# Differential attention on one core: two maps on the two halves of the array, one pass over the probabilities, the 16 prefix keys as a full chunk

## The chip, the cores and the metric

The kernel runs on one core of a Trainium2 chip. The metric is the device time of one execution in microseconds (us). TensorE (PE in the rows) does the matrix products, and its weight loads are listed apart as PEld; VectorE is DVE, ScalarE is ACT, GpSimd is POOL, SyncE is SP. The time before is 3174.17 us, the median of three runs.

## The reference, cut to what matters

The program is a hybrid block of three kinds of attention with a convolutional feed-forward layer, followed by two layers of a second kind. Each of the two layers has a SwiGLU, a mixing sublayer and another SwiGLU. The change touches the mixing sublayer's differential attention, on 16 prefix ("meta") tokens and 512 tokens, four heads, two maps of 64 features per head and values of 128 features:

```
s = einsum('bhmid,bhmjd->bhmij', q, k) * scale      # m = 0, 1: the two maps
p = softmax(where(allowed, s, -1e30))               # causal
a = p[:, :, 0] - lam * p[:, :, 1]
o = einsum('bhij,bhje->bhie', a, v)
o = o * rsqrt(mean(o * o) + EPS) * subln_w * (1 - lambda_init)
```

## The kernel before

The program is written against a layer that places buffers, adds the semaphores and puts the instructions of each engine in an order of its own: an instruction goes into its engine's order when, by that planner's own clock, its operands and its buffer are there, and among those that are ready the one written earlier in the program goes first. So matrix products written later (the projections of the next heads) are placed between the attention's own steps wherever those wait. Once the order is fixed, each engine takes its instructions in it.

PSUM has eight banks, in four rings: four banks "g" (projections), two "s" (scores), one "t" (transposes) and one "o" (outputs of the values' product).

`mix` handles a layer's mixing sublayer. It computes the four heads' values (`v_heads`, `v_major`), and then for b = 0 and 1 the queries and keys of two heads each: `gemm` (L172) makes a projection from exact high and low parts of both operands, with three products for each row block of 128 and the tokens in two segments of 264 (of one segment of 512 for the last layer's queries); `rotate` applies the rotary table; `stack` cuts the result into parts. Each b ends with `diff_heads` over its two heads, so that there are four such stages in the program, two for each layer. After them come the retention heads' projections, which are also L172.

`stack` makes tiles for products that are 128 deep. For map m (64 rows) the queries' high part and low part lie one above the other; for the keys the high part lies there twice, and one more tile holds the low parts of both maps. So a map's scores are one product 128 deep (L1466) and one 64 deep (L1467).

`diff_block` treats 128 queries (block b = 1 to 4, with 16 + 128 b keys; b = 0 is the 16 prefix tokens, which the last layer leaves out). For each map: the two products, the causal mask added by an identity product in bf16 (L1469), the row maximum (L1471), its scaling (L1476), the exponential with row sums (L1478). Block 4 has 528 keys, over the 512 of a bank, so its keys are taken in two spans of 264, each with a bank and the two products. Then two reciprocals (L1484, L1485), a pass that scales map 1 (L1486) and one that combines the maps (L1489). `yield`s part the steps: the generator of `diff_heads` writes scores(i + 1), transposes(i), values(i - 1). The transposes of the chunks of 128 keys go to bank "t" (L1496) and are copied in one piece (L1497); the 16 prefix keys are transposed into bank "o" (L1500) and copied apart (L1501). The values' product takes the chunks 128 deep (L1503), the prefix keys 16 deep (L1504); in f32 each of these is two matmul instructions. L1505 copies the result out and L1507 sums its squares.

Over the program there are 8 heads of a layer: 24 blocks b = 1 to 3, 8 blocks b = 4, and 4 blocks b = 0.

Of the kernel before, what the change touches and what calls it, by code (L numbers as in the profile page):

```python
# [10 lines left out]
F32 = mybir.dt.float32  # L11
# [54 lines left out]
class Weights:  # L66
    """[128, 512] tiles (high, low) of a [K, c] block, 512 / c rows of 128 in each"""
# [17 lines left out]
class QWeights:  # L85
    """tiles of the quarters (column tile n, rows k < 4 or k >= 4)"""
# [8 lines left out]
class Builder:  # L95
# [80 lines left out]
    def strassen_y(self, ys, R, keep=False):  # L176
        """the sums of the quarters of y (rows k < 4 and k >= 4, first and second half of the tokens)"""
# [17 lines left out]
    def gemm_pairs(self, W, ys, R, use, between=()):  # L195
        """all column tiles; the first two advance together, as the last of ys may come late"""
# [24 lines left out]
    def y_sums(self, T, k, a, c, w, q4, pool=None):  # L221
        """a and c: the rows k < 4 and k >= 4 of the first half of the tokens; w: both of the second half"""
# [25 lines left out]
    def strassen(self, src, Y, R, out, last, off=0, mid=None):  # L248
        """[2 * 128 features, tokens] of a block of weights with seven products of quarters (Winograd's form);
        the last product lies among the next block's, and last takes what it gives"""  # L250
# [15 lines left out]
        def product(i, ps=None, tag="g"):  # L266
            """with ps, added to what is there"""
# [59 lines left out]
    def sumsq(self, acc, src, R, k):  # L327
        """acc += src^2"""
# [27 lines left out]
    def bcast(self, rc, R):  # L356
        """rc, a column for each chunk of tokens, as rows in all partitions"""
# [34 lines left out]
    def prenorm_r(self, R):  # L392
        """the reciprocal of the norm, in all partitions"""
# [24 lines left out]
    def halves(self, parts, products, post, nextw, nparts=None):  # L418
        """the last products before a norm, half of the tokens by half; the second half is normalised in the next phase"""
# [53 lines left out]
    def bias_table(self, kind):  # L473
        """each row 128 times, to be read along its diagonals"""
# [22 lines left out]
    def band_head(self, qT, kT, base, kbase, V, bias, ops, obase, negm, l, sink=None):  # L497
        """q^T, k^T [64 rows, 512] in natural order; V(kb) the [128, 64] block; previous and own block."""
# [36 lines left out]
    def block_head(self, qT, kT, base, V, bias, ops, negm, l):  # L535
        """four independent 128-blocks"""
# [28 lines left out]
    def v_direct(self, W, ys, rcol, d):  # L565
        """values token-major: block b holds tokens b*128.. (d=1) or b::4 (d=4)"""
# [15 lines left out]
    def v_transposed(self, vTs, bufs=3):  # L582
        """[128 features, 512] tiles -> token-major blocks"""
# [82 lines left out]
    def gates(self, Y, gates):  # L666
        """the gates' products, kept in DRAM until the branches are merged"""
# [11 lines left out]
    def post_tile(self, ps, acc, t, R, add):  # L679
        """collects a tile of the sublayer's output, in the place of x, and its squares"""  # L680
# [8 lines left out]
    def postnorm(self, acc, gpost, R, Rn, xold, xnew):  # L689
        """x = xold + norm(x); the next pre-norm of the tokens Rn"""  # L690
# [186 lines left out]
    def stick_pair(self, q, k, V, t, ops, tri, cm):  # L877
        """two heads; the blocks j of 128 keys against the queries from j*128 on lie one after the other"""
# [71 lines left out]
    def conv_ffn(self):  # L950
# [5 lines left out]
        def conv(u, j):  # L956
            """u holds two zeros before the first token"""
# [84 lines left out]
    def last_w(self, src, nk=4, spare=("t3",)):  # L1042
        """nk rows of 128 for all columns, in two blocks; what the ring doesn't hold lies where the sums of y were"""
# [19 lines left out]
    def ffn_order(self, chunks, up, down, last):  # L1063
        """the down products of a chunk lie between the up products of the next one"""
# [15 lines left out]
    def flush(self):  # L1080
        """the elementwise rest of a block follows the products of the next one"""
# [4 lines left out]
    def hidden(self, src, dst):  # L1086
        """the parts of two hidden tiles"""
# [7 lines left out]
    # ---------------------------------------------------------------- block 2  # L1095
# [91 lines left out]
    def first_blocks(self, name, ys, R, gs):  # L1187
        """the first blocks in halves of the tokens, so that the second half has time to be normalised"""
# [27 lines left out]
    def mix(self, l, R):  # L1216
# [3 lines left out]
        with self.phase(f"mx{l}") as qp:  # L1220
# [22 lines left out]
            for b in range(2):  # L1243
                wq = wi(2 + 2 * b)
                q = [self.stack(self.rotate(self.gemm(wq, n, ys, R), rot, True), R, False) for n in range(2)]
# [3 lines left out]
                k = [self.stack(self.rotate(self.gemm(wk, n, ys, R2), rot, True), R2, True) for n in range(2)]  # L1249
# [74 lines left out]
    def feature_major(self, o, base, R):  # L1324
        """transposes [tokens, 128] blocks; yields (psum, first token, tokens) within the range R"""
# [27 lines left out]
    def lam(self, l):  # L1353
        nc = self.nc
# [9 lines left out]
        nc.vector.scalar_tensor_tensor(out=e[:, 2:3], in0=e[:, 0:1], scalar=li, in1=e[:, 1:2], op0=ALU.add, op1=ALU.subtract)  # L1364
# [32 lines left out]
    def stack(self, t, R, key):  # L1397
        """the two maps' exact parts for products of K = 128: the queries' high and low parts against the keys' high
        part twice, and the high part against the keys' low part"""
        nc = self.nc  # L1400
        s = slice(R.off, R.off + R.n)
        r = [slice(0, 64), slice(64, P)]
        out = [self.tmp("qk2", 10, dt=F32R) for _ in range(2)]
# [299 lines left out]
```

## Time and profile before

| | us |
|---|---|
| median of the three runs (lowest, highest) | 3174.17 (3173.94, 3175.4) |
| the profiled execution's span, first to last instruction | 3173.5 |
| PE busy in it | 3105.4 |
| DVE busy | 2250.6 |
| ACT busy | 1533.8 |

The profiled execution shows its span; the time of a run is what lies between its first and last instruction and a little around them, and the median of the runs is 0.7 us over this span. Busy time of PE counts an instruction from its start to its modelled end, and a matmul's end lies after the next one's start, so that a lost tenth of a microsecond between two matmuls does not show as idle time. It shows in the distance from one start to the next, which the timeline gives.

### The profile page before, as it was taken

To read this page: it belongs to the slowest core of one execution; us is meant where nothing else is said; L and a number is where in the kernel's file an instruction comes from. 1 tells how busy PE (TensorE), PEld (TensorE's weight loads), DVE (VectorE), ACT (ScalarE), POOL (GpSimd) and SP (SyncE) were. 2 spreads that over 40 slices of the span, in tenths; PEclk is the share of its full clock that TensorE was granted. 3 is DMA by queue.
4 is the path that set the end of the run, shared out by engine and by line. 5 is a ranking of instruction groups with operands and counts; after the bars stand their busy time and mean duration, and the time that the engine had idled before them with its cause. 6 is when DMAs were issued, how large, how long until landed. Compare 5 with 4: busy or idle time off the path is not lost.

```text
span 3173.5 us, 54811 instructions
## 1 busy us (share of the span) xinstructions
PE 3105.4 (98%) x22264; PEld 2872.8 (91%) x22264; DVE 2250.6 (71%) x4225; ACT 1533.8 (48%) x2968; POOL 0.7 (0%) x6
## 2 busy tenths in 40 slices
PE   5899999999999999999999999999999999999998
PEld 4676798988899999999889999999999988899998
DVE  4235777887888797775766777768777576677775
ACT  3345555665455554444553444445444455344443
POOL 0000000000000000000000000000000000000000
PEclk8899999999999999999999999999999999999999
DMA  4421236423233332333212223333233321223332
GB/s 120 95 78 62 81 123 204 145 87 111 89 102 110 102 107 94 107 98 104 66 52 64 87 88 106 94 100 94 94 107 95 107 67 59 67 84 106 96 108 77
DMA packets 102148, 304.36 MB, mean 96 GB/s; under 512 B 12387, under 2 KB 27367, under 8 KB 101896
## 3 DMA queue, kind: packets, MB, share of 16 engines
q1 hardware_dynamic: 98296, 294.38, 30.0%
q10 hardware_dynamic: 3600, 6.49, 0.7%
q8 instruction: 174, 2.85, 0.4%
q14 instruction: 78, 0.64, 0.1%
HBM read 286.41 MB, written 14.42 MB: 95 GB/s over the span
## 4 chain that ended last, share of the span: by engine, by line
PE 93%; DMA 4%; DVE 2%; ACT 1%; issue 0%; SPq 0%; DVEq 0%; ACTq 0%
PE ps_g L172 35%; PE ps_g L278 18%; PE ps_g L276 9%; PE ps_s L172 8%; PE ps_g L206 7%; PE ps_o L276 4%; PE ps_o L206 1%; DMA fd<-row 1%; PE ps_g L576 1%; DMA wraw<-in_w_in 1%; PE ps_s L1467 1%; DMA tmp_bias<-fd 1%; PE ps_s L510 1%; PE ps_s L1524 1%; PE ps_o L1503 1%; PE ps_o L532 1%
## 5 line engine op out<-in xcount | busy, mean ns | idle before, releaser
L140 DVE TENSOR_TENSOR wqL<-wraw,wqH 128x512 fp32r<-128x512 f32 (+1 forms) x676 | 604.8, 910 | 275.3 <-ACT wqH L139 267.4
L139 ACT CAST wqH<-wraw 128x512 fp32r<-128x512 f32 (+1 forms) x676 | 526.7, 796 | 495.6 <-PE ps_g L172 258.6
L172 PE MATMUL ps_g<-yH,wqH 128*128 128x264 f32 (+2 forms) x1520 | 430.4, 322 | 2.3 <-ACT wqH L139 2.2
L172 PE MATMUL ps_g<-yL,wqH 128*128 128x264 f32 (+2 forms) x1520 | 430.8, 321 | 0.4 <-DVE yL L414 0.4
L172 PE MATMUL ps_g<-yH,wqL 128*128 128x264 f32 (+2 forms) x1520 | 430.3, 322 | 0.8 <-DVE wqL L140 0.7
L278 PE MATMUL ps_g<-t,wqH 128*128 128x256 f32 (+1 forms) x1760 | 326.5, 283 | 0.0
L172 PEld LDWEIGHTS ps_g<-yL,wqH 128*128 128x128 f32 x1520 | 264.7, 189 | 24.9 <-issue 5.2
L172 PEld LDWEIGHTS ps_g<-yH,wqL 128*128 128x128 f32 x1520 | 263.1, 189 | 23.4 <-issue 4.1
L172 PEld LDWEIGHTS ps_g<-yH,wqH 128*128 128x128 f32 x1520 | 263.4, 189 | 22.6 <-ACT wqH L139 3.1
L278 PEld LDWEIGHTS ps_g<-t,wqH 128*128 128x128 f32 x1760 | 272.4, 188 | 1.8
L278 PE MATMUL ps_g<-t,wqL 128*128 128x256 f32 (+1 forms) x880 | 248.7, 283 | 0.0
L139 ACT CAST wqH<-ws 128x1024 fp32r<-128x1024 f32 x100 | 105.2, 1052 | 126.8 <-PE ps_o L276 34.3
L278 PEld LDWEIGHTS ps_g<-t,wqL 128*128 128x128 f32 x880 | 166.1, 189 | 0.0
L276 PE MATMUL ps_g<-t,wqH 128*128 128x264 f32 (+1 forms) x800 | 148.5, 283 | 0.0
L172 PE MATMUL ps_s<-hL,wqH 128*128 128x264 f32 (+1 forms) x544 | 141.4, 317 | 0.0
L172 PE MATMUL ps_g<-hL,wqH 128*128 128x264 f32 (+1 forms) x544 | 141.3, 317 | 0.0
L172 PE MATMUL ps_g<-hH,wqL 128*128 128x264 f32 (+1 forms) x544 | 141.2, 317 | 0.0
L172 PE MATMUL ps_s<-hH,wqL 128*128 128x264 f32 (+1 forms) x544 | 141.2, 317 | 0.0
L172 PE MATMUL ps_g<-hH,wqH 128*128 128x264 f32 (+1 forms) x544 | 141.1, 317 | 0.0
L172 PE MATMUL ps_s<-hH,wqH 128*128 128x264 f32 (+1 forms) x544 | 141.0, 317 | 0.0
L258 DVE TENSOR_TENSOR ws<-wraw 128x512 f32<-128x512 f32 x100 | 69.3, 693 | 86.9 <-DMA wraw<-in_ffn_w_gate 34.7
L140 DVE TENSOR_TENSOR wqL<-ws,wqH 128x1024 fp32r<-128x1024 f32 x100 | 122.4, 1224 | 6.6 <-ACT wqH L139 3.1
(434 smaller groups left out, 8207.9 us busy)
## 6 DMA issues: line engine op xcount, KB each, us to landing
wraw<-in_ffn_w_gate SPq DMA_DIRECT2D x88, 512.0 KB, 3.7
wraw<-in_ffn_w_up SPq DMA_DIRECT2D x88, 512.0 KB, 3.7
wraw<-in_ffn_w_down SPq DMA_DIRECT2D x88, 512.0 KB, 3.5
wraw<-in_w_in SPq DMA_DIRECT2D x86, 512.0 KB, 3.8
wraw<-in_w_up SPq DMA_DIRECT2D x64, 512.0 KB, 3.7
wraw<-in_w_down SPq DMA_DIRECT2D x32, 512.0 KB, 3.5
wraw<-in_w_gate SPq DMA_DIRECT2D x24, 512.0 KB, 4.1
tmp_p<-gates ACTq DMA_DIRECT2D x24, 256.0 KB, 3.6
```

The lines of the kernel that those rows point to most:

```text
L139: self.nc.scalar.copy(out=H, in_=raw)
L140: self.nc.vector.tensor_sub(out=L, in0=raw, in1=H.bitcast(F32))
L172: self.nc.tensor.matmul(t[:, :m], lhsT=a, rhs=b[:, o:o + m], start=(k == 0 and i == 0), stop=(k == nk - 1 and i == 2))
L206: self.nc.tensor.matmul(q[:, :m], lhsT=a, rhs=b[:, o:o + m], start=(k == 0 and i == 0), stop=(k == nk - 1 and i == 2))
L258: nc.vector.tensor_add(out=S[:, :512], in0=A21, in1=A22)
L276: nc.tensor.matmul(ps, lhsT=a, rhs=b, start=first, stop=last)
L278: nc.tensor.matmul(ps, lhsT=a, rhs=b, start=False, stop=last, skip_group_check=True)
L510: nc.tensor.matmul(ps[:, c], lhsT=q[:, i * P:(i + 1) * P], rhs=k[:, lo * P:(i + 1) * P], start=True, stop=True)
L532: nc.tensor.matmul(ops[obase:obase + 64, i * P:(i + 1) * P], lhsT=V(kb), rhs=pT[:, s0:s0 + P], start=(kb == lo), stop=(kb == i))
L576: nc.tensor.matmul(ps[:, :256], lhsT=a[:, ts], rhs=w, start=(k == 0 and i == 0), stop=(k == KD - 1 and i == 2))
L1467: nc.tensor.matmul(ps[:nq, :e - a], lhsT=qm[r], rhs=k[2][r, a:e], start=False, stop=not dg)
L1503: nc.tensor.matmul(ops[:nq, :P], lhsT=aT[:, j * P:j * P + nq], rhs=V[:, j], start=(j == 0), stop=False)
```

## The change

- `parts` takes the place of `stack`: a tile of high parts and one of low parts for queries and for keys, map 0 in rows 0 to 63 and map 1 in rows 64 to 127, each made by one instruction of ACT and one of DVE over all 128 rows. The queries are multiplied by the scale there.
- The scores of a map are three products 64 deep. The program writes them by turns for the two maps: high by high for map 0, then for map 1, low by high for both, high by low for both; the masks of both come after them.
- Block 4's spans are 512 keys and the 16 prefix keys. The first takes the two banks "s", the second two banks of the ring "g".
- Both row maxima are taken with a negated output, so that the scaling instruction goes; the combination of the spans' maxima and sums and the reciprocals treat both maps in one instruction.
- The maps are combined in one pass, a = p0 - (lam * l0 / l1) * p1, with l the row sums, and the result is divided by l0 when it leaves PSUM.
- The prefix keys become a chunk of 128 whose values are zero beyond row 15 (`memset` on POOL in `v_major`); it is the first 128 columns of the probabilities, transposed with the others into bank "t" and copied in the same piece (for block 4 into bank "o", copied apart).

```diff
-                q = [self.stack(self.rotate(self.gemm(wq, n, ys, R), rot, True), R, False) for n in range(2)]
+                q = [self.parts(self.rotate(self.gemm(wq, n, ys, R), rot, True), R, SCALE) for n in range(2)]
...
-                k = [self.stack(self.rotate(self.gemm(wk, n, ys, R2), rot, True), R2, True) for n in range(2)]
+                k = [self.parts(self.rotate(self.gemm(wk, n, ys, R2), rot, True), R2) for n in range(2)]
...
+    def parts(self, t, R, scale=None):
+
+        H, L = [self.tmp("qk2", 10, dt=F32R) for _ in range(2)]
+        self.split(t, H, L, R.off, R.n, scale)
+        return H, L
...
         out = self.qp.tile([P, 5, P], F32, name="vh", tag="vh", bufs=6)
+        nc.gpsimd.memset(out[:, 4], 0.0)
...
-        spans = [(0, nk)] if nk <= 512 else [(0, nk // 2), (nk // 2, nk)]
+        spans = [(0, nk)] if nk <= 512 else [(NMETA, nk), (0, NMETA)]
...
+        for i, (a, e) in enumerate(spans):
+            ps = [self.psum("sg"[i])[:nq, :e - a] for _ in range(2)]
+            for j, (x, y) in enumerate(((0, 0), (1, 0), (0, 1))):
+                for m in range(2):
+                    nc.tensor.matmul(ps[m], lhsT=q[x][r[m], qs], rhs=k[y][r[m], a:e], start=(j == 0),
+                                     stop=(j == 2 and i == 1))
+            if i == 0:
+                for m in range(2):
+                    nc.tensor.matmul(ps[m][:, e - a - nq:], lhsT=self.identb[:nq, :nq], rhs=self.dm[:nq, :nq],
+                                     start=False, stop=True)
+            pst.append(ps)
+        for i, ps in enumerate(pst):
+            for m in range(2):
+                c = 2 * i + m
+                nc.vector.tensor_reduce(out=sm[:nq, c:c + 1], in_=ps[m], axis=AX.X, op=ALU.max, negate=True)
...
+        nc.vector.reciprocal(out=sm[:nq, 8:10], in_=sm[:nq, 4:6])
+        nc.vector.scalar_tensor_tensor(out=sm[:nq, 10:11], in0=sm[:nq, 4:5], scalar=sm[:nq, 9:10], in1=lam[:nq],
+                                       op0=ALU.mult, op1=ALU.mult)
         a = Pm[0]
-        nc.vector.scalar_tensor_tensor(out=a[:nq, :nk], in0=a[:nq, :nk], scalar=sm[:nq, 8:9], in1=Pm[1][:nq, :nk],
-                                       op0=ALU.mult, op1=ALU.subtract)
+        nc.vector.scalar_tensor_tensor(out=a[:nq, :nk], in0=Pm[1][:nq, :nk], scalar=sm[:nq, 10:11], in1=a[:nq, :nk],
+                                       op0=ALU.mult, op1=ALU.add)
...
-                nc.tensor.transpose(pt[:, j * P:j * P + nq], a[:nq, NMETA + j * P:NMETA + (j + 1) * P], self.ident[:nq, :nq])
-            nc.scalar.copy(out=aT[:, :b * P], in_=pt[:, :b * P])
+                nc.tensor.transpose(pt[:, j * P:(j + 1) * P], a[:, NMETA + j * P:NMETA + (j + 1) * P], self.ident)
+            if b < 4:
+                nc.tensor.transpose(pt[:, b * P:(b + 1) * P], a[:, :P], self.ident)
+            n = min(b + 1, 4) * P
+            nc.scalar.copy(out=aT[:, :n], in_=pt[:, :n])
...
-        nc.tensor.matmul(ops[:nq, :P], lhsT=aT[:16, 4 * P:4 * P + nq], rhs=V[:16, 4], start=(b == 0), stop=True)
-        nc.vector.tensor_copy(out=o_sb[:nq, b], in_=ops[:nq, :P])
+        kk = 16 if b == 0 else P
+        nc.tensor.matmul(ops[:nq, :P], lhsT=aT[:kk, m], rhs=V[:kk, 4], start=(b == 0), stop=True)
+        nc.vector.tensor_scalar(out=o_sb[:nq, b], in0=ops[:nq, :P], scalar1=sm[:nq, 8:9], scalar2=None, op0=ALU.mult)
```

## Rows read from the trace of the kernel before

**Rows 1.** The page: busy time by engine, granted clock, chain that ended last.
```profile
PE 3105.4 (98%) x22264; PEld 2872.8 (91%) x22264; DVE 2250.6 (71%) x4225; ACT 1533.8 (48%) x2968; POOL 0.7 (0%) x6
...
PEclk8899999999999999999999999999999999999999
...
PE 93%; DMA 4%; DVE 2%; ACT 1%; issue 0%; SPq 0%; DVEq 0%; ACTq 0%
```

**Rows 2.** Windows: stretch, length, busy and (instructions) of PE, PEld, DVE, ACT, POOL; clock, DMA.
```profile
1495.00:1532.50 37.50, 37.50 (x316) 37.42 (x314) 21.86 (x37) 14.88 (x27) 0.00 (x0) 1.00 0.25 85
1532.50:1587.00 54.50, 54.17 (x366) 44.69 (x365) 44.39 (x138) 35.34 (x108) 0.00 (x0) 1.00 0.18 58
1587.00:1640.00 53.00, 53.00 (x358) 43.35 (x358) 36.70 (x127) 28.87 (x104) 0.00 (x0) 1.00 0.14 43
...
2564.40:2615.00 50.60, 50.49 (x299) 39.95 (x297) 41.26 (x118) 32.93 (x95) 0.00 (x0) 1.00 0.19 63
2615.00:2665.00 50.00, 50.00 (x332) 40.96 (x331) 32.84 (x106) 26.19 (x89) 0.00 (x0) 1.00 0.12 38
```

**Rows 3.** Timeline of PE around block 4's scores of map 1: start, length, instruction.
```profile
1608.35 0.40 PE L172 MATMUL ps_g<-yH,wqL 128*128 128x264 f32 x2
1608.59 0.28 PE L172 MATMUL ps_g<-yH,wqH 128*128 128x264 f32 x1
1608.71 0.28 PE L1466 MATMUL ps_s<-tmp_qk,tmp_qk 128*128 128x264 f32 x1
1608.92 0.39 PE L1467 MATMUL ps_s<-tmp_qk,tmp_qk 64*128 64x264 f32 x1
1609.24 0.39 PE L172 MATMUL ps_g<-yH,wqH 128*128 128x264 f32 x1
1609.46 0.28 PE L172 MATMUL ps_g<-yL,wqH 128*128 128x264 f32 x1
1609.58 0.28 PE L1466 MATMUL ps_s<-tmp_qk,tmp_qk 128*128 128x264 f32 x1
```

**Rows 4.** Timeline of PE: transposes, and a block's values with the 16-deep product.
```profile
1552.62 0.66 PE L1503 MATMUL ps_o<-vh,tmp_aT 128*128 128x128 f32 x4
1553.21 0.48 PE L1504 MATMUL ps_o<-vh,tmp_aT 16*128 16x128 f32 x2
1553.62 0.51 PE L172 MATMUL ps_g<-yH,wqL 128*128 128x264 f32 x2
1553.97 0.41 PE L172 MATMUL ps_g<-yH,wqH 128*128 128x264 f32 x2
...
1555.07 0.49 PE L1496 MATMUL ps_t<-ident,tmp_P 128*128 128x128 f32 x3
1555.40 0.27 PE L1500 MATMUL ps_o<-ident,tmp_P 128*16 128x128 f32 x1
```

**Rows 5.** Timeline of PE in the first block: 64-deep products of heads on alternate halves.
```profile
164.57 1.71 PE L543 MATMUL ps_s<-qk 64*128 64x128 f32 x16
166.50 1.16 PE L543 MATMUL ps_s<-qk 64*128 64x128 f32 x8 [0.23 <-DVE tmp_p L545]
```

**Rows 6.** Timeline of ACT: the exponentials that free the banks of rows 3.
```profile
1607.52 0.46 ACT L1478 ACTIVATE tmp_P<-ps_s,sm 128x264 f32<-128x264 f32 x1
...
1607.97 0.47 ACT L1478 ACTIVATE tmp_P<-ps_s,sm 128x264 f32<-128x264 f32 x1
```

**Rows 7.** One line's instructions: the projection's evacuation by ACT and DVE, the 64-deep weight loads.
```profile
L1385 ACT COPY tmp_t<-ps_g x28: 351/378/587, 1514.8 to 2615.2; 128x264 f32<-128x264 f32 x24, 128x512 f32<-128x512 f32 x4
...
L1392 DVE TENSOR_TENSOR tmp_sg<-ps_g,rot x28: 411/424/674, 1515.2 to 2618.0; 128x264 f32<-128x264 f32 x24, 128x512 f32<-128x512 f32 x4
...
L1467 PEld LDWEIGHTS ps_s<-tmp_qk,tmp_qk x88: 88/183/184, 1532.7 to 2655.5; 64*128 64x128 f32 x80, 64*16 64x16 f32 x8
```

**Rows 8.** Groups by line, 1532 to 1640 us, and POOL's memset in the whole program.
```profile
L1471 DVE TENSOR_REDUCE sm<-ps_s 128x1 f32<-128x264 f32 (+4 forms) x48 | 18.6, 388 | 13.6 <-PE ps_s L1469 10.0 <-PE ps_s L1467 3.4
...
L1486 DVE TENSOR_SCALAR tmp_P<-tmp_P,sm,lame 16x16 f32<-16x16 f32 (+4 forms) x20 | 8.2, 412 | 0.2
...
L1407 ACT CAST tmp_qk<-tmp_sg 64x528 fp32r<-64x528 f32 x11 | 6.9, 631 | 3.2 <-DVE tmp_sg L1394 3.0
...
masks.py:197 POOL MEMSET ident<- 128x128 f32 x1 | 0.2, 204 | 0.3 <-POOLq L1692 0.3
```

More of the change, by code (lines that the diff above doesn't have):

```diff
@@ L1363, in lam @@
         nc.scalar.activation(out=e[:, :2], in_=ps[:, :2], func=AF.Exp)
[L1364 removed]
+        nc.vector.scalar_tensor_tensor(out=e[:, 2:3], in0=e[:, 1:2], scalar=-li, in1=e[:, 0:1], op0=ALU.add, op1=ALU.subtract)
         return e[:, 2:3]
@@ L1395, in rotate @@
         return out
[L1397 to L1403, printed above, removed]
-        low = self.tmp("qk2", 10, dt=F32R) if key else None
-        for m in range(2):
-            a, b = r[m], r[1 - m]
-            nc.scalar.copy(out=out[m][a, s], in_=t[a, s])
-            if key:
-                nc.scalar.copy(out=out[m][b, s], in_=t[a, s])
-            nc.vector.tensor_sub(out=low[a, s] if key else out[m][b, s], in0=t[a, s], in1=out[m][a, s].bitcast(F32))
-        return (*out, low) if key else out
+    def parts(self, t, R, scale=None):
+        H, L = [self.tmp("qk2", 10, dt=F32R) for _ in range(2)]
+        self.split(t, H, L, R.off, R.n, scale)
+        return H, L
     def v_heads(self, ps, rb, c0):
@@ L1455, in diff_block @@
         nk = NMETA + b * P
-        spans = [(0, nk)] if nk <= 512 else [(0, nk // 2), (nk // 2, nk)]
-        sm = self.sp.tile([P, 10], F32, name="sm", tag="sm", bufs=4)
-        Pm = []
+        spans = [(0, nk)] if nk <= 512 else [(NMETA, nk), (0, NMETA)]
+        sm = self.sp.tile([P, 12], F32, name="sm", tag="sm", bufs=4)
+        r = [slice(64 * m, 64 * m + 64) for m in range(2)]
+        qs = slice(q0, q0 + nq)
+        pst = []
+        for i, (a, e) in enumerate(spans):
[9 more added lines that the diff above has]
+            pst.append(ps)
@@ L1459, in diff_block @@
+        for i, ps in enumerate(pst):
+            for m in range(2):
+                c = 2 * i + m
+                nc.vector.tensor_reduce(out=sm[:nq, c:c + 1], in_=ps[m], axis=AX.X, op=ALU.max, negate=True)
+        if len(spans) == 2:
+            nc.vector.tensor_tensor(out=sm[:nq, 0:2], in0=sm[:nq, 0:2], in1=sm[:nq, 2:4], op=ALU.min)
+        Pm = [self.tmp("P", 4) for _ in range(2)]
         for m in range(2):
-            qm, km, r = q[m][:, q0:q0 + nq], k[m], slice(64 * m, 64 * m + 64)
@@ L1461, in diff_block @@
-            p = self.tmp("P", 4)
-            pst = []
             for i, (a, e) in enumerate(spans):
-                ps = self.psum("s")
-                dg = e == nk
-                nc.tensor.matmul(ps[:nq, :e - a], lhsT=qm, rhs=km[:, a:e], start=True, stop=False)
-                nc.tensor.matmul(ps[:nq, :e - a], lhsT=qm[r], rhs=k[2][r, a:e], start=False, stop=not dg)
-                if dg:
-                    nc.tensor.matmul(ps[:nq, e - a - nq:e - a], lhsT=self.identb[:nq, :nq], rhs=self.dm[:nq, :nq],
-                                     start=False, stop=True)
-                nc.vector.tensor_reduce(out=sm[:nq, i:i + 1], in_=ps[:nq, :e - a], axis=AX.X, op=ALU.max)
-                pst.append(ps)
@@ L1495, in diff_block @@
             for j in range(b):
-                nc.tensor.transpose(pt[:, j * P:j * P + nq], a[:nq, NMETA + j * P:NMETA + (j + 1) * P], self.ident[:nq, :nq])
-            nc.scalar.copy(out=aT[:, :b * P], in_=pt[:, :b * P])
+                nc.tensor.transpose(pt[:, j * P:(j + 1) * P], a[:, NMETA + j * P:NMETA + (j + 1) * P], self.ident)
[3 more added lines that the diff above has]
+            nc.scalar.copy(out=aT[:, :n], in_=pt[:, :n])
         yield
         ops = self.psum("o")
-        nc.tensor.transpose(ops[:16, P:P + nq], a[:nq, :16], self.ident[:nq, :nq])
-        nc.scalar.copy(out=aT[:16, 4 * P:4 * P + nq], in_=ops[:16, P:P + nq])
+        m = slice(b * P, b * P + nq)
+        if b == 4:
+            nc.tensor.transpose(ops[:, P:2 * P], a[:, :P], self.ident)
+            nc.scalar.copy(out=aT[:, m], in_=ops[:, P:2 * P])
+        elif b == 0:
+            nc.tensor.transpose(ops[:16, P:P + nq], a[:nq, :16], self.ident[:nq, :nq])
+            nc.scalar.copy(out=aT[:16, m], in_=ops[:16, P:P + nq])
         for j in range(b):
-            nc.tensor.matmul(ops[:nq, :P], lhsT=aT[:, j * P:j * P + nq], rhs=V[:, j], start=(j == 0), stop=False)
-        nc.tensor.matmul(ops[:nq, :P], lhsT=aT[:16, 4 * P:4 * P + nq], rhs=V[:16, 4], start=(b == 0), stop=True)
-        nc.vector.tensor_copy(out=o_sb[:nq, b], in_=ops[:nq, :P])
+            nc.tensor.matmul(ops[:nq, :P], lhsT=aT[:, j * P:(j + 1) * P], rhs=V[:, j], start=(j == 0), stop=False)
+        kk = 16 if b == 0 else P
+        nc.tensor.matmul(ops[:nq, :P], lhsT=aT[:kk, m], rhs=V[:kk, 4], start=(b == 0), stop=True)
+        nc.vector.tensor_scalar(out=o_sb[:nq, b], in0=ops[:nq, :P], scalar1=sm[:nq, 8:9], scalar2=None, op0=ALU.mult)
         sq = self.qp.tile([P, P], F32, name="sqd", tag="sqd", bufs=1)
```

20 lines of the change are left out of this document (5 added, 15 removed).

## The prediction

> **What bounds the kernel now.** I read the page first: PE is busy for 98% of the span at the full granted clock, and the chain that ended last runs through PE for 93% [rows 1]. So the question is how much of PE's time the change touches, and whether that time is work or loss. Busy time can't say, so I took the windows of the four attention stages (two lie in each layer, 208 us in all). PE is busy in all of them, yet its instructions stand further apart: 316 in the 37.5 us before the first stage, which is 0.119 us each, against 0.148 us in the second stage (358 in 53.0), although many of the stage's products are shorter. DVE and ACT are busy for 36.7 and 28.9 us of those 53 [rows 2]: neither sets the pace.
>
> The timeline shows the loss. Projection products of 264 columns start 0.12 us apart (two from 1608.35 to 1608.59) [rows 3]. Around a 64-deep product they don't: the four products from 1608.59 to 1609.46 take 0.87 us where 0.48 would do. So a trip from 128-deep products to a 64-deep one and back costs 0.39 us. The 16-deep values cost the same: 1552.62 to 1553.97 holds six products of 128 f32 columns and two of 264; at 0.11 us for one of the former (three transposes, 1555.07 to 1555.40) and 0.12 for the latter that is 0.90 us, and it took 1.35, so 0.45 for the trip [rows 4]. I take 0.40 us a trip. The Trainium skill says the same in kind (TensorEngine Tiling (Array Packing), Key Properties: a change of tiling mode drains the engine); it gives no price, so the sum has only the rows'.
>
> A block b = 1 to 3 makes three such trips now (one for each map's scores, one for its prefix values), block 4 makes five. That is 24 × 3 + 8 × 5 = 112, or 45 us, and some more in the four blocks b = 0.
>
> **The values.** Padded to 128, the prefix chunk makes no trip: 32 × 0.40 = -12.8 us. Its two matmuls stay, and so does its transpose, which is 128 columns of f32 in either shape. In block 0 the two maps' scores go together and save a trip: 4 × 0.40 = -1.6 us; the ends are nothing and twice that.
>
> **The scores.** Three 64-deep products for each map stand where one 128-deep and one 64-deep were. Two things decide: whether the two maps run at once on the two halves, and whether they stand together, so that they share one trip.
>
> That halves do run at once is in the trace, in another kind of attention: eight 64-deep products take 1.16 us, and sixteen, of two heads on the two halves, take 1.71 [rows 5]. Eight more cost 0.55 us, not 0.9. So I take the second map as free where both are ready.
>
> Whether they stand together depends on the banks. Each block needs both "s" banks, and the exponentials of the block before free them one after the other: 0.45 us apart for 264 columns [rows 6]. Just behind those two rows, the same two banks get products 0.87 us apart with two projection products between [rows 3], although nothing but the banks held the second. The planner thus fills a bank when it comes free, and will issue map 0's three products before map 1's bank is there, unless the three take longer than the gap. From 0.12 us for 264 columns I estimate 0.065, 0.124, 0.18 and 0.23 us for 144, 272, 400 and 512 columns. Three of these are 0.20, 0.37, 0.54 and 0.69 us. The gaps before them come from the block before, whose exponentials are 128 columns narrower: some 0.45 us for 264, by the same slope 0.35 for 144 and 0.55 for 400; block 1 follows block 4 (0.6 us or more) or block 0. So block 1 comes apart, block 2 is a toss-up, blocks 3 and 4 hold together, with the maps in sequence rather than by turns, so that they overlap by half: 4.5 products' time.
>
> In one trip and by turns, a block's columns take three products' time instead of four; apart, six.
> - Block 1 apart: 8 × 2 × 0.065 = +1.0 us.
> - Block 2, half of either: 8 × (-0.40 - 0.124 + 0.248) / 2 = -1.1 us.
> - Block 3: 8 × (-0.40 + 0.5 × 0.18) = -2.5 us.
> - Block 4: four trips become two (one for each span), and eight products of 264 (0.96 us) become 4.5 of 512 and six of 16 columns. A 16-column product is between 0.01 us by its columns and the 0.11 of the nearest row [rows 4]; I take 0.03 for each, 0.18 in all. 8 × (-0.80 + 4.5 × 0.23 + 0.18 - 0.96) = -4.4 us; at 0.11 each it is 3.8 us less gain.
>
> **Banks of the ring "g".** Block 4's second span holds two of the four from its scores to its exponentials, so a two-segment projection that ends meanwhile has no banks for its successor until its own are evacuated: two copies of 0.38 us and two products of 0.42 in parallel, with signals some 1 to 1.5 us [rows 7]. Nothing of it happens now. Eight such holds cost between 0 and 12 us. PE has attention work ready in most of them, and many holds will not meet the end of a projection: I take 0.3 us each, +2.4 us.
>
> **Edits costed at nothing.** DVE loses a pass of 0.41 us and small instructions for each block [rows 8], ACT four of six 0.63 us casts for each head [rows 8], and reductions stay. PE covers it: DVE's 36.7 us leave 16 us of room in the second stage [rows 2], so all this would be worth something only if PE lost over a quarter of its time there. The `memset` is 0.2 us on POOL, which does nothing else in that stretch [rows 1, 8]; the copy into the slot's 16 rows now waits for it, and only the next values on ACT stand behind that copy, projections ahead of their use. The ring of `parts` holds eight tiles instead of ten for each b, which only loosens. A block now needs its scores, two reductions and two exponentials before the next one's scores: some 0.6 + 0.8 + 0.9 us and the signals, about 3 us; ten blocks in a stage need 30 us of its 50, so the chain stays hidden as long as projections are there to fill.
>
> **Sum.** -12.8 - 1.6 + 1.0 - 1.1 - 2.5 - 4.4 + 2.4 = -19.0 us. Against the profiled span of 3173.5 that is 3154.5, and with the 0.7 us between it and the median of the runs 3155.2 us.
>
> **Rivals.**
> - *All pairs form.* The planner's gap is shorter than I think, or an order by turns survives. Then trips and columns pay in full: -12.8 - 1.6, blocks 1 to 3 24 × -0.40 and 8 × -(0.065 + 0.124 + 0.18) = -12.6, block 4 8 × (-0.80 + 3 × 0.23 + 0.18 - 0.96) = -7.1, no holds: -34.1, 3140 us. For it speaks that gap and triple are near each other in three blocks; against it rows 3.
> - *No pair forms; the scores don't do what the change says.* Each map's three products go alone: blocks 1 to 3 8 × 2 × 0.369 = +5.9, block 4 no trip saved and 8 × (6 × 0.23 + 0.18 - 0.96) = +4.8; with the values, block 0 and the holds -1.3: 3173 us, no change that shows. Rows 3 speak for it.
> - *The holds of "g" stall the projections in full*: 12 us instead of 2.4, -9.4: 3165 us. What now stands idle on PE gives no sign of such a shortage either way.
> - *The other side: loads laid bare.* If a 64-deep product can't load its weights while its own half computes, each second and third product of a map that goes alone waits for its load, 0.183 us [rows 7]. Apart, 32 blocks × 2 maps × 2 and the 32 of the 16-column triples make 160 waits, 29 us on top of -1.3: 3202 us. It decides for slower from 0.05 us a wait. The Trainium skill has it so (TensorE: Matmul & The Clock Gate, Part 3: a load overlaps matmuls in flight only on another row group). By that rule this rival's sum would stand wherever the maps come apart. Rows 5 speak against it: eight on one half in 1.16 us leave no room for bare loads, if f32 there behaves like the exact parts here.
>
> **How the numbers follow.** A difference under 0.2%, 6.3 us, can't be told from no change in this kernel. Chances: the forecast 0.50, all pairs 0.20, no pairs 0.13, holds 0.10, bare loads 0.07. Faster takes the first two and the holds, 0.80; same is the case without pairs, 0.13; slower is the bare loads, 0.07. The range reaches from a little under the case of all pairs to the case of none: 3137 to 3173 us, which leaves out the bare loads and the far tails of the others. The forecast by itself is good for 3147 to 3163.
>
> **What would show it.** Right: no 16-deep product but block 0's; fewer than 60 trips; the four stages together some 19 us shorter and everything after them as long as now; in blocks 3 and 4 products of the two halves starting within 0.02 us of each other; in block 1 two bouts of scores with projections between. Wrong, towards more gain: pairs in every block. Wrong, towards less: L172's products idle before a start around block 4, waiting for an evacuation; starts of one map's products 0.2 us and more apart; or a stage after the attention that grew because the planner ordered it otherwise, which no row here can tell.

## The result, and the profile after

| | before | after |
|---|---|---|
| median of 4 runs each, us (lowest, highest) | 3174.36 (3173.94, 3175.4) | 3206.24 (3205.59, 3206.28) |
| ratio to before, 95% interval | | 1.0098 [1.0087, 1.011] |
| the profiled execution's span, us | 3173.5 | 3204.4 |
| granted clock over the span | 0.989 | 0.974 |

The kernel became 32 us slower, where 19 us less were forecast. The page of the changed kernel, the lines that answer to [rows 1]:

```profile
PE 3122.2 (97%) x22352; PEld 2892.2 (90%) x22352; DVE 2228.3 (70%) x4085; ACT 1512.1 (47%) x2912; POOL 3.5 (0%) x22
...
PEclk8799999999999999999889999999999988999999
...
PE 93%; DMA 3%; DVE 2%; ACT 1%; issue 0%; SPq 0%; DVEq 0%; ACTq 0%
```

DVE and ACT have less to do, as the change wanted, and PE is still nearly the whole chain. What is new are the two dents in the line of the clock, at slices 20 and 21 and 33 and 34: the attention of the two layers. The windows of the four stages, with the projections between the two stages of the first layer as the third row (columns as in [rows 2]):

```profile
1495.00:1533.50 38.50, 38.50 (x324) 38.28 (x324) 21.30 (x35) 12.61 (x24) 0.00 (x0) 1.00 0.24 83
1533.50:1579.00 45.50, 40.00 (x250) 32.00 (x250) 27.43 (x83) 23.45 (x88) 0.41 (x2) 0.77 0.07 24
1579.00:1594.30 15.30, 15.30 (x130) 15.16 (x130) 10.70 (x18) 5.91 (x12) 0.00 (x0) 1.00 0.20 70
1594.30:1641.00 46.70, 43.10 (x253) 33.62 (x253) 25.10 (x79) 20.68 (x82) 0.00 (x0) 0.74 0.09 29
...
2581.50:2620.00 38.50, 33.64 (x193) 26.03 (x193) 25.00 (x69) 20.34 (x71) 0.41 (x2) 0.82 0.08 28
...
2635.50:2677.00 41.50, 37.30 (x202) 29.18 (x202) 22.25 (x64) 18.88 (x68) 0.00 (x0) 0.71 0.10 33
```

Before, the four stages held 1355 products in 208.1 us, 0.154 us each, PE never idle for long and the clock at 1.00 [rows 2]. Now they hold 898 in 172.2 us, 0.192 us each. PE is idle for 18.2 us of them, and the granted clock is 0.71 to 0.82. There are 457 fewer though the attention has 88 more of its own (264 score products where there were 176): so 545 others are missing, 527 of them L172's projections (741 before, 214 now). They come later, as in the third row, at 0.118 us each and the full clock. So the attention runs without its filler.

The first stage shows how. The timeline of PE:

```profile
1533.48 0.23 PE L1458 MATMUL ps_s<-tmp_qk,tmp_qk 64*16 64x16 f32 x6
1533.65 0.20 PE L1462 MATMUL ps_s<-dm,identb 16*16 16x16 bf16 x2
1533.77 0.50 PE L1458 MATMUL ps_g<-tmp_qk,tmp_qk 64*128 64x16 f32 x6
1536.72 1.16 PE L1458 MATMUL ps_s<-tmp_qk,tmp_qk 64*128 64x144 f32 x6 [2.44 <-ACT tmp_P L1475]
1537.82 0.40 PE L1462 MATMUL ps_s<-dm,identb 128*128 128x128 bf16 x2
1538.90 0.19 PE L1502 MATMUL ps_o<-ident,tmp_P 16*16 16x16 f32 x1 [0.69 <-DVE tmp_P L1483]
1539.08 0.59 PE L1458 MATMUL ps_g<-tmp_qk,tmp_qk 64*128 64x16 f32 x4
...
1556.00 0.59 PE L172 MATMUL ps_g<-yH,wqH 128*128 128x264 f32 x1
1556.39 0.42 PE L172 MATMUL ps_g<-yL,wqH 128*128 128x264 f32 x1
1556.61 0.42 PE L172 MATMUL ps_g<-yH,wqL 128*128 128x264 f32 x1
```

Everything that touches a bank of ring "g" in this stage except projections, by line (x: how often; first and last start in us):

```profile
L1458 PE MATMUL ps_g<-tmp_qk,tmp_qk x12: 252/315/379, 1533.8 to 1541.1; 64*128 64x16 f32 x12
...
L1468 DVE TENSOR_REDUCE sm<-ps_g x4: 164/166/167, 1548.4 to 1567.9; 128x1 f32<-128x16 f32 x4
L1475 ACT ACTIVATE tmp_P<-ps_g,sm x4: 259/267/275, 1554.7 to 1573.5; 128x16 f32<-128x16 f32 x4
```

Block 4's prefix products, 16 columns wide, are not issued when block 4's turn comes, but as soon as their keys are there: head 0's at 1533.77, head 1's from 1539.08 to 1541.1. Their exponentials come with block 4: head 0's from 1554.7, head 1's up to 1573.5. From 1539.1 on all four banks of the ring are held, until head 0's two come free near 1556, and between the last projection product at 1533.3 and 1556.00 there is not one of L172; before, the trace has 104 of them from 1534 to 1556. PE waits for exponentials (2.44 us at the first place), and at 1536.9 the granted clock falls to 0.50, the lower of its two levels (1.2 GHz, against 2.4 before):

```profile
1537.50:1557.00 19.50, 16.98 (x73) 12.60 (x72) 9.84 (x32) 8.52 (x35) 0.00 (x0) 0.50 0.05 16
```

That is the window over the stretch. In it a projection product takes 0.22 us from start to start (1556.39 to 1556.61) where [rows 3] have 0.12. The four stages lose the clock for 20.5, 23.9, 13.7 and 23.9 us, 82 us together.

How long PE waits at the first hole is not set by the exponentials' own length. In the fourth stage block 1's scores and masks are through at 2636.3, and this follows:

```profile
2636.45 1.23 DVE L140 TENSOR_TENSOR wqL<-wraw,wqH 128x1024 fp32r<-128x1024 f32 x1 [1.04 <-ACT wqH L139]
...
2638.90 0.70 DVE L1394 TENSOR_TENSOR tmp_t<-tmp_t,rot 128x528 f32<-128x528 f32 x1
2639.52 0.30 DVE L1468 TENSOR_REDUCE sm<-ps_s 128x1 f32<-128x144 f32 x1
2639.86 0.38 ACT L1475 ACTIVATE tmp_P<-ps_s,sm 128x144 f32<-128x144 f32 x1 [2.88 <-DVE sm L1468]
2640.38 1.04 PE L1458 MATMUL ps_s<-tmp_qk,tmp_qk 64*128 64x272 f32 x3 [3.67 <-ACT tmp_P L1475]
```

The row maximum (L1468) stands on DVE behind the weights' low parts (L140) and the rotation of the last projection (up to L1394); ACT waits 2.88 us for it and PE 3.67. In the first stage 1.28 of the 2.44 us are ACT's load of the exponential's table (1535.01 to 1536.29). The kernel before has the same load at the same place (1534.92), and there projections run under it.

### The profile page after: what moved, and what is told of

It is laid out like the page before. It is cut to its first block, busy times and chain, and to the rows that moved or that the text cites. A ratio compares the mean times of both kernels' runs of the same rounds, so it can differ in the third digit from the quotient of the medians.

```text
span 3204.4 us, 54842 instructions
## 1 busy us (share of the span) xinstructions
PE 3122.2 (97%) x22352; PEld 2892.2 (90%) x22352; DVE 2228.3 (70%) x4085; ACT 1512.1 (47%) x2912; POOL 3.5 (0%) x22
## 4 chain that ended last, share of the span: by engine, by line
PE 93%; DMA 3%; DVE 2%; ACT 1%; issue 0%; SPq 0%; DVEq 0%; ACTq 0%
PE ps_g L172 34%; PE ps_g L278 18%; PE ps_g L276 9%; PE ps_s L172 8%; PE ps_g L206 7%; PE ps_o L276 4%; PE ps_s L1458 1%; PE ps_o L206 1%; DMA fd<-row 1%; PE ps_g L576 1%; DMA tmp_bias<-fd 1%; PE ps_o L532 1%; PE ps_s L510 1%; PE ps_o L1505 1%; PE ps_s L1527 1%; DMA tmp_p<-gates 1%
## 5 line engine op out<-in xcount | busy, mean ns | idle before, releaser
L140 DVE TENSOR_TENSOR wqL<-wraw,wqH 128x512 fp32r<-128x512 f32 (+1 forms) x676 | 604.9, 910 | 294.4 <-ACT wqH L139 286.8
L172 PE MATMUL ps_g<-yH,wqH 128*128 128x264 f32 (+2 forms) x1520 | 428.0, 321 | 0.1
L172 PE MATMUL ps_g<-yH,wqL 128*128 128x264 f32 (+2 forms) x1520 | 426.8, 320 | 0.3 <-DVE wqL L140 0.2
L172 PE MATMUL ps_g<-yL,wqH 128*128 128x264 f32 (+2 forms) x1520 | 424.8, 319 | 0.4 <-DVE yL L414 0.4
L172 PEld LDWEIGHTS ps_g<-yL,wqH 128*128 128x128 f32 x1520 | 263.8, 189 | 23.1 <-issue 4.9
L172 PEld LDWEIGHTS ps_g<-yH,wqL 128*128 128x128 f32 x1520 | 263.0, 189 | 21.1 <-issue 4.1
L172 PEld LDWEIGHTS ps_g<-yH,wqH 128*128 128x128 f32 x1520 | 263.5, 190 | 18.3 <-ACT tmp_p L485 0.7
L172 PE MATMUL ps_s<-hL,wqH 128*128 128x264 f32 (+1 forms) x544 | 141.2, 317 | 0.0
L172 PE MATMUL ps_g<-hL,wqH 128*128 128x264 f32 (+1 forms) x544 | 141.2, 317 | 0.0
L172 PE MATMUL ps_g<-hH,wqL 128*128 128x264 f32 (+1 forms) x544 | 141.1, 317 | 0.0
L172 PE MATMUL ps_s<-hH,wqL 128*128 128x264 f32 (+1 forms) x544 | 141.1, 317 | 0.0
L172 PE MATMUL ps_g<-hH,wqH 128*128 128x264 f32 (+1 forms) x544 | 141.0, 317 | 0.0
L172 PE MATMUL ps_s<-hH,wqH 128*128 128x264 f32 (+1 forms) x544 | 140.9, 316 | 0.0
L140 DVE TENSOR_TENSOR wqL<-ws,wqH 128x1024 fp32r<-128x1024 f32 x100 | 122.3, 1223 | 6.4 <-ACT wqH L139 2.6
```

Of the source, the lines that this page charges most:

```text
L172: self.nc.tensor.matmul(t[:, :m], lhsT=a, rhs=b[:, o:o + m], start=(k == 0 and i == 0), stop=(k == nk - 1 and i == 2))
```

## The experiments

For every kernel I counted, from the trace: the trips to 64- or 16-deep products in the four stages, the time at the half clock in them, PE's idle time in them, and two sums of start-to-start distances of PE: "attention", all of the time from a layer's first score to its last copy of an output, less 0.12 us for each projection product in it; and of that "scores", the distances behind score products and masks alone.

| kernel | median, us (runs) | ratio to before, 95% | trips | half clock, us | idle, us | attention, us | scores, us |
|---|---|---|---|---|---|---|---|
| before | 3174.36 (4) | | 123 | 0 | 0.4 | 118.7 | 51.4 |
| after | 3206.24 (4) | 1.0098 [1.0087, 1.011] | 54 | 82.0 | 18.2 | 149.7 | 76.1 |
| e1 | 3239.07 (2) | 1.0198 [1.0179, 1.0216] | 56 | 146.8 | 26.5 | 182.2 | 90.9 |
| e2 | 3165.15 (5) | 0.9965 [0.9951, 0.9978] | 71 | 0 | 3.0 | 110.4 | 45.3 |
| e3 | 3229.10 (2) | 1.0166 [1.0148, 1.0185] | 122 | 99.0 | 15.6 | 170.0 | 90.4 |
| e4 | 3163.01 (5) | 0.9957 [0.9945, 0.997] | 92 | 0 | 0.5 | 107.2 | 51.5 |
| e5 | 3165.93 (5) | 0.9969 [0.9956, 0.9981] | 76 | 0 | 2.4 | 109.5 | 48.2 |
| e6 | 3160.01 (5) | 0.9950 [0.9938, 0.9963] | 76 | 0 | 2.2 | 105.9 | 41.0 |
| e7 | 3175.37 (11) | 1.0006 [0.9996, 1.0015] | 92 | 0 | 0.6 | 117.4 | 58.3 |
| e8 | 3174.59 (11) | 0.9996 [0.9987, 1.0004] | 123 | 0 | 0.2 | 118.4 | 50.8 |
| e9 | 3158.40 (5) | 0.9941 [0.9929, 0.9954] | 61 | 0 | 5.1 | 102.5 | 36.0 |
| e10 | 3203.54 (5) | 1.0078 [1.0065, 1.0092] | 70 | 71.7 | 14.4 | 147.7 | 78.3 |

The difference of "attention" to before gives the time of every kernel within some 4 us, so little outside the stages matters. The ratios were taken against runs of the kernel before made beside each kernel, with medians from 3174.4 to 3177.1 us. Line numbers in the rows are those of each kernel.

**e1, the prefix products put off.** The changed kernel, with the second span queued on PE behind the first span's masks.

```diff
+            with self.tc.issue_after(last.ins) if last else ExitStack():
                 for j, (x, y) in enumerate(((0, 0), (1, 0), (0, 1))):
...
-                    nc.tensor.matmul(ps[m][:, e - a - nq:], lhsT=self.identb[:nq, :nq], rhs=self.dm[:nq, :nq],
+                    last = nc.tensor.matmul(ps[m][:, e - a - nq:], lhsT=self.identb[:nq, :nq], rhs=self.dm[:nq, :nq],
```

> The kernel after, with block 4's prefix span (16 keys, two banks of ring g) put behind the masks of its first span in PE's order. Theory R (the ring g is handed out in the order in which the program writes its tiles, so projections written later can't have a bank before block 4 of the heads before them has given its own back): nothing is mended, 3195 to 3220 us, no projection products between the attention's steps of the first head, and a clock as low as after (0.97). Theory H (the prefix products are issued as soon as their operands are there and so hold two to four banks through the stage): with the early issue gone the projections come back, 3150 to 3165 us, clock 0.99. Theory C (64-deep products by themselves let the clock fall): 3200 to 3210 us.

It became worse, 3239 us, which is theory R's sign and above its range. What starts in ring "g" on PE between 1532 and 1556 us, by line:

```profile
L172 PE MATMUL ps_g<-yH,wqL x6: 280/282/284, 1531.9 to 1533.5; 128*128 128x264 f32 x6
L1460 PE MATMUL ps_g<-tmp_qk,tmp_qk x6: 357/358/380, 1550.6 to 1551.1; 64*128 64x16 f32 x6
```

The prefix products now start at 1550.6, as they were told to, and still no projection stands between 1533.5 and them. So it isn't only that filled banks are held. Banks of a ring go out in the order in which the program writes their tiles: a projection that is written after block 4's second span gets no bank before that span has got its own, though all four banks lie empty once the last projection has been read out of them at 1537.2. This goes with e1's being slower than the changed kernel: head 1's span is issued at 1574.0, and the first projection after 1533.5 starts at 1576.8, where the changed kernel has one at 1556.00.

**e3, the kernel before with that ring alone.** Block 4's second span of 264 keys takes its bank from ring "g"; nothing else is changed.

```diff
-                ps = self.psum("s")
+                ps = self.psum("sg"[i])
```

> The kernel before, with nothing changed but the bank of block 4's second span: ring g in place of s, for both maps. R: projections are shut out until the first head's block 4 is through, PE idles, the clock falls in the four stages, 3185 to 3215 us. C: no 64-deep pairs here, so no change, 3170 to 3178 us. H: slower too, but less than after, since a map's span is issued when its operands come, 3180 to 3200 us.

The loss is there in full, and above theory R's range: 3229 us, with 99 us at the half clock and 15.6 us of PE idle. The first stage's timeline and window:

```profile
1534.97 0.23 PE L1469 MATMUL ps_g<-dm,identb 128*128 128x128 bf16 x1
1537.12 0.33 PE L1466 MATMUL ps_s<-tmp_qk,tmp_qk 128*128 128x144 f32 x1 [1.92 <-ACT tmp_P L1478]
```
```profile
1532.00:1586.00 54.00, 49.15 (x240) 35.81 (x239) 34.94 (x121) 29.28 (x99) 0.00 (x0) 0.75 0.06 20
```

This kernel has no pair of half-array products, no padded chunk and the old passes: the ring alone makes the loss and the fall of the clock.

**e2 and e5, the change without ring "g".** In e2 block 4 goes map by map in two spans of 264 keys in ring "s", with three 64-deep products for each. In e5 only the source of two banks is changed: the prefix span takes "t" for map 0 and "o" for map 1.

```diff
# e2
-        spans = [(0, nk)] if nk <= 512 else [(NMETA, nk), (0, NMETA)]
+        spans = [(0, nk)] if nk <= 512 else [(0, nk // 2), (nk // 2, nk)]
...
+        for ms in [(0, 1)] if b < 4 else [(0,), (1,)]:
...
+                ps = {m: self.psum("s")[:nq, :e - a] for m in ms}
# e5
-            ps = [self.psum("sg"[i])[:nq, :e - a] for _ in range(2)]
+            ps = [self.psum(("ss", "to")[i][m])[:nq, :e - a] for m in range(2)]
```

> The kernel after, with block 4 taken map by map in two spans of 264 in the ring s, as before, so that the scores use no bank of ring g; products stay 64 deep, all else as after. R and H: projections stand between the attention's steps again, no clock fall in the four stages, 3145 to 3165 us. C: the clock still falls there and the time stays above 3195 us.

> The kernel after, with the two banks of block 4's prefix span taken from the rings t (map 0) and o (map 1) in place of ring g; nothing else. R: the projections have ring g to themselves again, no clock fall in the four stages, 3145 to 3165 us, the loss of the change gone. A rival to R (it is the length of block 4's hold of any bank, or the 512-column span, that stalls): the time stays above 3190 us.

Both recover 40 us: 3165 and 3166 us, just over the top edge of what was expected, with no fall of the clock. L172's products of e5 from 1537 to 1556 us, where the changed kernel has none:

```profile
L172 PE MATMUL ps_g<-yH,wqH x26: 281/285/391, 1537.2 to 1555.6; 128*128 128x264 f32 x26
L172 PE MATMUL ps_g<-yL,wqH x24: 279/283/369, 1537.6 to 1553.9; 128*128 128x264 f32 x24
L172 PE MATMUL ps_g<-yH,wqL x24: 278/284/391, 1537.8 to 1554.9; 128*128 128x264 f32 x24
```

The windows of e5's first two stages (columns as in [rows 2]):

```profile
1537.00:1583.00 46.00, 45.25 (x349) 39.01 (x350) 35.44 (x98) 27.16 (x96) 0.41 (x2) 1.00 0.15 47
1583.00:1634.00 51.00, 50.35 (x377) 42.37 (x376) 31.89 (x93) 27.87 (x94) 0.00 (x0) 1.00 0.15 48
```

Between e5 and the changed kernel lie two banks for each head, and 40 us: 15.8 us more of idle PE (18.2 less 2.4), and by subtraction 24 us in the rest, where products were slower while the clock stood at half for 82 us.

**e10, half of the banks.** The prefix span of map 0 in ring "g", that of map 1 in "o".

```diff
-            ps = [self.psum("sg"[i])[:nq, :e - a] for _ in range(2)]
+            ps = [self.psum(("ss", "go")[i][m])[:nq, :e - a] for m in range(2)]
```

> The changed kernel with one bank of block 4's prefix span (map 0's) in the ring g and the other (map 1's) in the ring o: a stage takes two banks of ring g instead of four. Theory R (the loss is that projections cannot get a bank before block 4 has freed its own): the four banks of ring g serve two projections at a time, so with one tile for each head the next projection is still held, but one of two segments may go on; between the kernel with none in g (3166 us) and the one with two for each head (3206): 3172 to 3195 us, with stretches in which few projections stand on PE and the clock falls in some of the four stages. Rival (the loss comes with the clock alone, all or nothing): 3166 us with no fall of the clock, or 3206 with four.

I expected a loss between, and got nearly all of it, 3203.5 us with four falls of the clock: outside theory R's range, and near what the rival foretold. The timeline:

```profile
1533.45 0.50 PE L1458 MATMUL ps_g<-tmp_qk,tmp_qk 64*128 64x16 f32 x3
1536.40 0.80 PE L1458 MATMUL ps_s<-tmp_qk,tmp_qk 64*128 64x144 f32 x6 [2.45 <-ACT tmp_P L1475]
...
1538.76 0.59 PE L1458 MATMUL ps_g<-tmp_qk,tmp_qk 64*128 64x16 f32 x2
1539.29 0.81 PE L172 MATMUL ps_g<-yH,wqH 128*128 128x264 f32 x2
```

The first hole is the same. No projection goes before head 1's span, which starts at 1538.76. Then projections run again, but 37 products from 1534 to 1556 where the kernel before has 104: with two banks held, two are left, and one projection of two segments needs two. So the loss does not go by the number of banks held. Two things remain that no run parts: the first hole, which is as long as with four banks and which the clock's fall follows, and the second projection in flight, which has no banks afterwards.

**e4 and e8, parts of the change on the kernel before.** e4 has only the padded prefix chunk (L1423's `memset`, the chunk's transposes and values 128 deep); e8 only the single pass over the probabilities and the division on the way out of PSUM.

```diff
# e4
+        nc.gpsimd.memset(out[:, 4], 0.0)
...
-        nc.tensor.matmul(ops[:nq, :P], lhsT=aT[:16, 4 * P:4 * P + nq], rhs=V[:16, 4], start=(b == 0), stop=True)
+        nc.tensor.matmul(ops[:nq, :P], lhsT=aT[:kk, m], rhs=V[:kk, 4], start=(b == 0), stop=True)
# e8
-        nc.vector.tensor_scalar(out=Pm[1][:nq, :nk], in0=Pm[1][:nq, :nk], scalar1=sm[:nq, 9:10], scalar2=lam[:nq],
-                                op0=ALU.mult, op1=ALU.mult)
...
-        nc.vector.tensor_copy(out=o_sb[:nq, b], in_=ops[:nq, :P])
+        nc.vector.tensor_scalar(out=o_sb[:nq, b], in0=ops[:nq, :P], scalar1=sm[:nq, 8:9], scalar2=None, op0=ALU.mult)
```

> The kernel before, with the padded prefix chunk alone (zeroed slot, full transposes, 128-deep last product). The prediction's term: 32 trips of 0.40 us less, -12.8 us, 3159 to 3164 us. Rival: the lost tenths are hidden anyway, within 3 us of before.

> The kernel before with the single pass over the probabilities alone (both reciprocals in one instruction, lam * l0 / l1 on map 1, division by l0 on the way out of PSUM): DVE loses a pass of 0.41 us in each of 36 blocks. The prediction's term: nothing, within 3 us of before, as PE covers it. Rival: the attention's chain is on the path, 36 x 0.56 us = up to 20 us less.

e4 gains 13.6 us (0.0043 of 3174; the interval reaches from 9.5 to 17.5) with 31 trips fewer, 0.44 us each; by the sums of the two traces it is 11.5 us, 0.37 each. The timeline of a block's values and the next transposes in e4:

```profile
1548.52 0.38 PE L1512 MATMUL ps_o<-vh,tmp_aT 128*128 128x128 f32 x2
1548.74 0.39 PE L1514 MATMUL ps_o<-vh,tmp_aT 128*128 128x128 f32 x2
1548.96 0.38 PE L1497 MATMUL ps_t<-ident,tmp_P 128*128 128x128 f32 x2
```

The prefix values (L1514) follow the others after 0.22 us and take 0.22 for two products, 0.11 each: the trip of [rows 4] is gone. e8 changes nothing that can be told. ACT's fewer casts were not run alone.

**e7, the maps apart.** e5 with the products of map 0, its mask, then those of map 1, written so.

```diff
-            for j, (x, y) in enumerate(((0, 0), (1, 0), (0, 1))):
-                for m in range(2):
+            for m in range(2):
+                for j, (x, y) in enumerate(((0, 0), (1, 0), (0, 1))):
```

> The run with the prefix span in rings t and o, but each map's three products and its mask written as one piece, so that the maps come apart in every block. By the prediction's terms a block loses a trip (0.40 us) and up to three products' time: 5 to 20 us over the run with the prefix span in t and o. By bare weight loads (the prediction's rival): over 25 us more.

3175.4 us, 9.4 over e5 (its runs spread from 3171.8 to 3183.1, and the trace is of one at 3171.9): with most maps apart the scores cost 6.8 us more than those of e4, and eat half of what the values give. A bout of e7 that goes alone:

```profile
1539.95 0.81 PE L1458 MATMUL ps_s<-tmp_qk,tmp_qk 64*128 64x400 f32 x3
1540.69 0.23 PE L1461 MATMUL ps_s<-dm,identb 128*128 128x128 bf16 x1
```

Three products of 400 columns on one half take 0.74 us from the first's start to the mask's. At the prediction's 0.18 us each that is 0.54, and 0.2 are left for the changes of mode. Two bare loads of 0.183 would by themselves bring the products to 0.91. The third product's weight load shows it too: it runs from 1540.24 to 1540.42, under the second product (start 1540.23), and the third starts at 1540.42.

**e6 and e9, the pairs held together.** e6 is e5 with each of a block's six products queued behind the one before it, map 1 first. e9 is e5 with a wait: the first span's products start after the exponential that frees the second of the two banks.

```diff
+                    if i == 0 and self.freed:
+                        self.tc.add_manual_dep(mm.ins, self.freed.name, mybir.DependencyInfo(
+                            mybir.DependencyClass.Sync, mybir.DependencyReason.DATA), reason="both banks")
...
+                if i == 0 and m == 1:
+                    self.freed = act.ins
```

> The run before it (prefix span in rings t and o), with the scores' products held in one order, by turns and map 1 first, so that no block's maps come apart. If the halves overlap and a shared trip is worth what the prediction took, 24 blocks and 8 blocks 4 gain what was still apart: 5 to 15 us under the run before it, down to the prediction's case of all pairs, 3140 us. If holding the order costs more in waits than pairs give: the same or slower than the run before it.

> The changed kernel with block 4's prefix span in the rings t and o, and a real wait added: a block's score products start only when the last exponential of the block before (map 1's) has freed the second of the two banks, so that both maps' products stand side by side in one trip. Theory P (what the pairs are still short of is the 0.4 us of every trip that the planner leaves between the maps): fewer than 60 trips, no projection between the first and the last of a block's products, 76 - 55 = some 20 trips by 0.4 us less than the kernel with the prefix span in t and o alone: 3150 to 3160 us. Rival Q (a pair that waits for both banks holds PE's order, and what it gives back in trips it loses in waiting): trips under 60 too, but PE idle by 5 us and more in the stages and 3164 us or more.

e6 didn't hold the pairs: in 12 places a single product of 400 columns stands alone, and the trips stayed at 76. Even so it is 5.9 us faster than e5 (3160.0 against 3165.9), its scores 7.2 us shorter; why, with as many trips, is not shown. e9 held them: 28 of the 32 blocks b = 1 to 4 have their six products in one piece (nothing but masks and prefix products between), against 15 in e5. A pair of e9 on the timeline:

```profile
1541.19 0.40 PE L172 MATMUL ps_g<-yH,wqL 128*128 128x264 f32 x2
1541.53 0.65 PE L1460 MATMUL ps_s<-tmp_qk,tmp_qk 64*128 64x272 f32 x6
1542.11 0.29 PE L1467 MATMUL ps_s<-dm,identb 128*128 128x128 bf16 x2
1542.23 0.28 PE L1497 MATMUL ps_t<-ident,tmp_P 128*128 128x128 f32 x1
```

Six products and both masks in 0.70 us; before, the two maps' bouts of this block, 128 deep and 64 deep with a mask, took 0.63 us each on average. e9 is the fastest kernel of the study, 3158.4 us. Both theories came half true: 61 trips and not under 60, a time inside the range of the first, and the idle time of the second (5.1 us against 2.4 in e5). Its scores take 15.5 us less than those of e4, the attention only 4.7. The rest went into the projections among them, whose distances beyond 0.12 us grew from some 19 to 26 us, as PE waits behind them for the second bank and the change of mode, and into values and transposes. Between e4 (the padded chunk alone) and e9 the intervals overlap.

## Why the prediction was wrong, step by step

**The step that failed is the term of ring "g".** It says that block 4's second span holds two of four banks from its scores to its exponentials, that a projection then waits 1 to 1.5 us for its predecessor's evacuation, and "PE has attention work ready in most of them, and many holds will not meet the end of a projection: I take 0.3 us each, +2.4 us", with 12 us as the bound. It measured 40 us (3206.2 against e5's 3165.9). Three things in it were wrong. The hold doesn't begin with block 4's turn: the products are issued when their keys are there, 20 us ahead, for both heads of the stage, so that all four banks are gone. It doesn't even need the products: the ring's banks go out in written order (e1). And PE had no attention work ready: a block waits for its exponentials, and these for DVE's row maxima, so that without projections PE stands idle and the clock falls, which takes a projection from 0.12 to 0.22 us. The price of a hold was worked out from one evacuation where it had to be worked out from the length of the stage. The bound of 12 us, and with it the range and the rival's 3165 us, hung on the same step.

The prediction had the condition in another sentence: the chain of blocks stays hidden "as long as projections are there to fill". It asked whether DVE and ACT have room, not whether the change takes the filler away. The Trainium skill names the pressure (TensorEngine Tiling (Array Packing), Restrictions and Gotchas, Gotcha 1: row tiles write to different PSUM banks at once and need more of them); it gives no price. Block 4 in pairs does take four banks at once. But the 40 us are not the price of that pressure: e5 takes as many banks from other rings, and e3 loses more (52 us) without any pair. They are the price of taking them from the projections' ring.

**The values: right.** -12.8 us foretold, -13.6 measured (e4, interval -17.5 to -9.5); a trip costs 0.44 us by that, taken as 0.40.

**Edits of DVE and ACT at nothing: right as far as run.** e8, the single pass, is within 0.13% of before; the casts and the negated maxima were not run by themselves. What DVE and ACT have queued did cost time once the projections were gone.

**The scores: no gain shown.** Foretold were -8.6 us with block 0. e5 against e4 is +2.9 us by the medians (3165.9 and 3163.0), with intervals that overlap. This is not the term by itself, since e5 also takes the rings "t" and "o" for the prefix span; e2, which takes neither and goes map by map in block 4, stands at 3165.2. The guess which blocks hold together was off: of eight blocks each, four stood whole at 144 columns, four at 272, one at 400 and six at 512, where apart, half, together and together were foretold. So block 3 paid instead of gaining. And where pairs form, part of what they save returns as waiting around them (e9).

**The rivals.** "All pairs form" at 3140 us: not reached even where the pairs are made to stand (3158). "No pair forms" at 3173: e7, which writes the maps apart, gives 3175. "Bare loads" at 3202 comes near the measured time, and is not its cause: e7's bout leaves no room for them, and e5 has none of the loss. The Trainium skill's rule (TensorE: Matmul & The Clock Gate, Part 3) that a load overlaps only matmuls on another row group does not hold in that bout.

**What it named as signs.** No 16-deep product outside block 0: right. Fewer than 60 trips: right, 54, and no use, since it comes mostly from the missing projections, which no longer part the attention's steps (e5, with projections, has 76). The four stages are 36 us shorter and not 19, because projections left them. "L172's products idle before a start around block 4" was the sign named for less; what came was L172 missing for 22 us in the first stage.

## What to carry to other kernels

Where one engine bounds a kernel because filler work covers another chain's waits, ask of every new buffer: does the filler take from the same ring, in which order are that ring's buffers given out, and how long after the grant is the last reader? A tile that is written early and read late shuts out all that is written after it, however small it is. Price such a hold by the stage that runs bare, with the lower clock that may come with it, not by one evacuation.

## What the runs showed of the hardware that was not expected

- The granted clock fell to 0.50 (1.2 GHz) early in each stage that had lost its projections. In the changed kernel it fell 0.2 us behind a hole of 2.44 us and inside holes of 2.14, 3.71 and 3.67 us; in e10's second stage it fell 0.6 us behind one of 0.98 us. In the changed kernel it stayed there for 13.7 to 23.9 us of each stage with the attention's products going on, and projections took 0.22 us instead of 0.12. In e2 and e4 to e9, whose longest hole in a stage is 0.84 us, it fell in no stage.
- Six 64-deep products on both halves of the array take little longer than three on one: in e9 the six of 272 columns and two masks 0.70 us (median of eight, 0.67 to 1.09), in e7 three of 272 and one mask 0.61 us on average. Where e7 has all six in sequence, map by map with a mask between, they take 1.37 us.
